# Fixed SBUF addresses for the operands of TensorE's products in a two-layer hybrid encoder

## The chip, the cores and the metric

The kernel runs on one core of one Trainium2 chip. The metric is the device time of one execution, in microseconds (us). The kernel before took 1218.03 us, the median of 3 runs (1217.06 to 1219.15).

## The reference, cut to what matters

The program is an encoder of two layers on 512 tokens of 1024 features, all in float32. Layer 0 mixes tokens with windowed attention (8 query heads, 2 key heads), layer 1 with a recurrent block (convolution, two gated scans, GELU gate). After each mixer comes a squared-ReLU MLP, and every sub-layer is wrapped in a modulation computed from `c` and a LayerNorm:

```python
def sq_relu_mlp(h, w1, w2):
    return jnp.square(jax.nn.relu(h @ w1)) @ w2
...
    y = sq_relu_mlp(x * (1.0 + scale) + shift, mlp_w1[i], mlp_w2[i])
    x = layer_norm(DN_ALPHA * x + (1.0 + gate) * y, ln_g[i, 1], ln_b[i, 1])
```

The two MLPs (1024 to 4096 to 1024) are most of the arithmetic.

## The kernel before

**Products in three passes.** TensorE multiplies in a rounded form of float32 (fp32r), so every float32 operand is split into a high part and a low part, and `mm3` (line 604) issues three matmuls for one product: high by high, high by low, low by high. Each matmul has a stationary operand, `lhsT`, of 128 partitions by 128 columns, which an LDWEIGHTS instruction loads, and a moving operand, `rhs`, of 128 partitions by up to 512 columns, which the MATMUL streams. A column is 4 bytes in each partition.

**Buffers.** Per partition of SBUF there are six weight buffers `w0` to `w5` (2048 columns: high parts, then low parts), four `raw` buffers into which weights land by DMA, `ht` (8192 columns: the modulated activations, transposed), `hid0` to `hid15` (512 columns each, used in pairs, high and low: the hidden activations), `xb0` to `xb3`, `rows` (6144 columns), `acc2`, fifteen `ex` buffers for temporaries, and some tens of small tiles.

**Order of the work.** A weight unit is 128 by 1024 values. `dma_unit` (line 543) loads it on SP's queue into a raw buffer, `conv_unit` (line 554) splits it with one ScalarE cast and one VectorE subtraction into a free `w` buffer. `m_tiles` (line 854) multiplies a unit, stationary, by `ht`, moving: 8 products, 24 matmuls. `out_tiles` (line 875) multiplies `hid` (in the attention and the recurrent block partly `ht`), stationary, by a unit, moving: again 24 matmuls per unit. An MLP goes four times through 8 units of the first kind and 8 of the second. Beside the first MLP run the matrix-vector products of the modulations (`gemv_tasks`, line 696): DMAs into the same raw buffers and long VectorE instructions.

**Who sets the order.** The kernel is written as a list of operations on symbolic tiles; `schedule` (line 330) is a planner that gives every operation a cost and an engine and puts all in one static order. It knows tiles by name and size; no address enters it. `emit` (line 468) then issues the operations in that order, and `real` (line 476) makes the actual tile at the moment when an operation first names it.

**Where the buffers lie.** The pool hands out SBUF addresses in the order in which tiles are made, each rounded up to 32 bytes, from byte 16512 on, which is 128 modulo 256. Tiles are made on first use, so small tiles of 4 to 512 bytes fall in between the large ones, and the large ones land on different addresses modulo 256. In the program of the kernel before these are:

| buffer | address modulo 256 |
|---|---|
| ht | 0 |
| w0, w3, w4, w5 | 192 |
| w1 | 32 |
| w2 | 128 |
| hid0, hid1 | 96 |
| hid2, hid3 | 192 |
| hid4, hid5 | 224 |
| hid6 to hid15 | 0 |

All slices that the products take inside a buffer begin at multiples of 512 bytes, so the distance between two operands modulo 256 is that of their buffers. In what follows the **distance** of a matmul is the address of the stationary operand that is loaded next, less that of the moving operand that is being streamed, modulo 256. The matmuls of the program and of the trace stand in the same order, so each record can be given its operands' addresses (the trace's names leave the buffer numbers out). For 512-column matmuls of 128 partitions that ran at full clock, the distances are as follows; "w by ht" is w stationary and ht moving, "hid by w" hid stationary and w moving; stretches are us from the start of the span:

| stretch, product | 192 | 0 | 32 | 64 | 96 | 128 | 160 | 224 |
|---|---|---|---|---|---|---|---|---|
| 13.7 to 61, w by ht | 119 | 0 | 48 | 0 | 0 | 24 | 0 | 0 |
| 61 to 219, w by ht | 44 | 0 | 0 | 0 | 0 | 0 | 0 | 0 |
| 61 to 219, hid by w | 0 | 10 | 22 | 28 | 0 | 0 | 17 | 11 |
| 219 to 392.6, w by ht | 171 | 0 | 70 | 0 | 0 | 49 | 0 | 0 |
| 219 to 392.6, hid by w | 11 | 24 | 35 | 205 | 2 | 24 | 23 | 57 |
| 392.6 to 418.8, w by ht | 47 | 0 | 24 | 0 | 0 | 24 | 0 | 0 |
| 418.8 to 558.9, w by ht | 177 | 0 | 24 | 0 | 0 | 47 | 0 | 0 |
| 418.8 to 558.9, hid by w | 11 | 36 | 29 | 135 | 2 | 23 | 35 | 66 |
| 558.9 to 616, w by ht | 72 | 0 | 0 | 0 | 0 | 0 | 0 | 0 |
| 558.9 to 616, hid by w | 0 | 0 | 4 | 35 | 2 | 0 | 1 | 2 |
| 616 to 861.9, w by ht | 263 | 0 | 73 | 0 | 0 | 95 | 0 | 0 |
| 616 to 861.9, hid by w | 5 | 1 | 1 | 52 | 18 | 27 | 0 | 28 |
| 861.9 to 1199.1, w by ht | 404 | 0 | 120 | 0 | 0 | 120 | 0 | 0 |
| 861.9 to 1199.1, hid by w | 5 | 60 | 60 | 361 | 28 | 84 | 94 | 49 |

The functions that the change touches, with their line numbers:

Of the kernel before, what the change touches and what calls it, by code (L numbers as in the profile page):

```python
# [9 lines left out]
F32 = mybir.dt.float32  # L10
# [223 lines left out]
class Program:  # L234
# [233 lines left out]
    def emit(self, nc, tc, pools):  # L468
        fix = lambda a: self.real(a, pools)
        with tc.manual_schedule():  # L470
            for op in self.schedule():
                args = [fix(a) for a in op.args]
                kw = {k: fix(a) for k, a in op.kw.items()}
                op.ins = getattr(getattr(nc, op.eng), op.fn)(*args, **kw)  # L474

    def real(self, a, pools):
        if not isinstance(a, View):
            return a
        t = a.tile
        if t.real is None:  # L480
            pool = pools[t.kind]
            shape = [1, t.n] if t.kind == "dr" else [128, t.n]
            tag = f"ps{t.bank}" if t.kind == "ps" else t.tag
            t.real = pool.tile(shape, F32, tag=tag, name=tag)
        return a.get()
# [1027 lines left out]
```

## Time and profile before

| | before |
|---|---|
| median of 3 runs | 1218.03 us |
| the profiled execution's own time | 1218.25 us |
| its span (first to last instruction) | 1216.5 us |
| TensorE matmuls, busy | 1148.1 us (94%), 5332 of them |
| TensorE weight loads, busy | 938.8 us (77%), beside the matmuls |
| VectorE busy | 871.3 us (72%) |
| ScalarE busy | 529.3 us (44%) |

How to read it: the span is 1.75 us shorter than the execution's own time, so a change of the span is a change of the time. TensorE is busy most of the time, but a matmul is pipelined: its record overlaps the next one's, so the time that one costs is the distance from its start to the start of the next (called its pitch here), not the duration that a row gives as the mean of one. In a timeline row of N matmuls in one piece, the piece's length is N-1 pitches and one last record. All lines stand as L474, since one helper issues every operation; names of tiles tell the work apart, buffer numbers left out.

### The profile page before, as it was taken

To read this page: it belongs to the slowest core of one execution; us is meant where nothing else is said; L and a number is where in the kernel's file an instruction comes from. 1 tells how busy PE (TensorE), PEld (TensorE's weight loads), DVE (VectorE), ACT (ScalarE), POOL (GpSimd) and SP (SyncE) were. 2 spreads that over 40 slices of the span, in tenths; PEclk is the share of its full clock that TensorE was granted. 3 is DMA by queue.
4 is the path that set the end of the run, shared out by engine and by line. 5 is a ranking of instruction groups with operands and counts; after the bars stand their busy time and mean duration, and the time that the engine had idled before them with its cause. 6 is when DMAs were issued, how large, how long until landed. Compare 5 with 4: busy or idle time off the path is not lost.

```text
span 1216.5 us, 14406 instructions
## 1 busy us (share of the span) xinstructions
PE 1148.1 (94%) x5332; PEld 938.8 (77%) x5332; DVE 871.3 (72%) x1303; ACT 529.3 (44%) x787; POOL 77.1 (6%) x47
## 2 busy tenths in 40 slices
PE   7987989999999899998999988979999999999996
PEld 5876767988888688887887866768888888888885
DVE  7898979978878785449948888689935444444447
ACT  4465664512322342424468889834431422322411
POOL 1000000022232220000000000000000000000004
PEclk9997999999999999999999989899999999999998
DMA  9866552367667753221232442443422222222201
GB/s 337 297 193 206 157 181 79 117 220 247 204 239 244 240 192 138 87 104 37 96 104 92 143 130 84 148 139 101 164 100 102 89 101 90 101 90 95 96 1 70
DMA packets 54140, 172.01 MB, mean 141 GB/s; under 512 B 7715, under 2 KB 8227, under 8 KB 54070
## 3 DMA queue, kind: packets, MB, share of 16 engines
q1 hardware_dynamic: 54070, 171.09, 42.0%
q8 instruction: 42, 0.69, 0.2%
q14 instruction: 28, 0.23, 0.1%
HBM read 160.56 MB, written 2.11 MB: 134 GB/s over the span
## 4 chain that ended last, share of the span: by engine, by line
PE 63%; DVE 19%; ACT 8%; DMA 7%; issue 2%; SPq 0%; DVEq 0%; ACTq 0%
PE ps L474 63%; DVE ex L474 5%; DVE w L474 4%; DVE rows L474 3%; DMA raw<-in_adaw 3%; DVE xb L474 2%; ACT rows L474 2%; ACT w L474 2%; DMA raw<-in_W 1%; DVE ht L474 1%; DVE acc L474 1%; DMA rows<-w 1%; ACT ex L474 1%; ACT L474 1%; DVE mv L474 1%
## 5 line engine op out<-in xcount | busy, mean ns | idle before, releaser
L474 PE MATMUL ps<-ht,w 128*128 128x512 f32 (+1 forms) x2664 | 557.0, 370 | 6.2 <-ACT w L474 3.9
L474 PEld LDWEIGHTS ps<-ht,w 128*128 128x128 f32 x2664 | 461.8, 190 | 96.6 <-ACT w L474 4.4
L474 PE MATMUL ps<-w,hid 128*128 128x512 f32 (+1 forms) x1800 | 422.7, 393 | 0.0
L474 DVE TENSOR_TENSOR w<-raw,w 128x1024 fp32r<-128x1024 f32 x192 | 240.5, 1257 | 228.9 <-ACT w L474 226.2
L474 PEld LDWEIGHTS ps<-w,hid 128*128 128x128 f32 x1800 | 335.7, 189 | 78.8 <-DVE rows L474 0.2
L474 ACT CAST w<-raw 128x1024 fp32r<-128x1024 f32 x192 | 198.6, 1042 | 429.7 <-PE ps L474 304.2
L474 PE MATMUL ps<-w,ht 128*128 128x512 f32 (+1 forms) x336 | 74.2, 371 | 6.3 <-DVE w L474 3.4
L474 PEld LDWEIGHTS ps<-w,ht 128*128 128x128 f32 x336 | 57.4, 193 | 18.2 <-DVE w L474 3.8
L474 DVE SCALAR_TENSOR_TENSOR ex<-rows,ps 128x512 f32<-128x512 f32 (+1 forms) x81 | 53.2, 672 | 22.0 <-PE ps L474 22.0
L474 DVE SCALAR_TENSOR_TENSOR acc<-raw,sc,acc 128x1024 f32<-128x1024 f32 x40 | 52.6, 1314 | 16.2 <-DMA raw<-in_adaw 15.9
L474 ACT ACTIVATE rows<-ps 128x512 f32<-128x512 f32 x66 | 39.1, 592 | 43.4 <-PE ps L474 41.9
L474 DVE SCALAR_TENSOR_TENSOR rows<-raw,sc,rows 128x1024 f32<-128x1024 f32 x40 | 53.8, 1346 | 4.9 <-DMA raw<-in_adaw 4.6
L474 DVE TENSOR_TENSOR xb<-xb,ex 128x512 f32<-128x512 f32 (+1 forms) x81 | 55.5, 698 | 0.6
L474 POOL TENSOR_TENSOR ex<-xb,rows 128x512 f32<-128x512 f32 x5 | 6.8, 1375 | 754.1 <-ACT xb L474 754.1
L474 DVE TENSOR_TENSOR hid<-ex,hid 128x512 fp32r<-128x512 f32 x66 | 47.5, 722 | 5.5 <-ACT hid L474 0.9
L474 DVE TENSOR_TENSOR ex<-rows 128x512 f32<-128x512 f32 x64 | 45.8, 715 | 5.4 <-ACT rows L474 5.4
L474 ACT ACTIVATE hid<-rows 128x512 fp32r<-128x512 f32 x64 | 40.5, 633 | 1.9
L474 PE MATMUL ps<-ex,w 96*128 96x512 f32 x108 | 31.5, 445 | 8.8 <-ACT ex L474 3.2
L474 PEld LDWEIGHTS ps<-ex,w 96*128 96x128 f32 x108 | 22.5, 214 | 16.8 <-ACT w L474 4.9
L474 DVE TENSOR_TENSOR rows<-rows,ex 128x512 f32<-128x512 f32 x32 | 21.6, 686 | 18.6 <-DMA rows<-rows 12.6
L474 ACT ACTIVATE xb<-xb,mv 128x512 f32<-128x512 f32 x29 | 22.2, 808 | 26.7 <-DVE mv L474 26.7
L474 PE MATMUL ps<-ident,ex 128*128 128x128 f32 x124 | 21.1, 285 | 10.9 <-DVE ex L474 9.8
(147 smaller groups left out, 830.0 us busy)
## 6 DMA issues: line engine op xcount, KB each, us to landing
raw<-in_W SPq DMA_DIRECT2D x184, 512.0 KB
raw<-in_adaw SPq DMA_DIRECT2D x80, 512.0 KB
ex<-in_ada0t SPq DMA_DIRECT2D x28, 256.0 KB
rows<-w SPq DMA_DIRECT2D x16, 192.0 KB
raw<-in_W SPq DMA_DIRECT2D x8, 288.0 KB
rows<-rows SPq DMA_DIRECT2D x36, 64.0 KB
xb<-in_xT SPq DMA_DIRECT2D x8, 256.0 KB
rows<-in_lnb SPq DMA_DIRECT2D x4, 512.0 KB
```

The source lines that it names most:

```text
L474: op.ins = getattr(getattr(nc, op.eng), op.fn)(*args, **kw)
```

## The change

Before it issues anything, the kernel now makes the large buffers in a fixed order, with three unused pads of 128, 192 and 192 bytes per partition between their groups. `place` looks up the first tile of each name in the planned order, and sets its `real`; `real()` finds it there later. Small tiles are made on first use as before, after all the large ones.

```diff
     def emit(self, nc, tc, pools):
         fix = lambda a: self.real(a, pools)
         with tc.manual_schedule():
-            for op in self.schedule():
+            order = self.schedule()
+            self.place(order, pools)
+            for op in order:
                 args = [fix(a) for a in op.args]
                 kw = {k: fix(a) for k, a in op.kw.items()}
                 op.ins = getattr(getattr(nc, op.eng), op.fn)(*args, **kw)
+
+    LAYOUT = (
+        [128, "ht", "rows", "acc2"]
+        + [f"ex{i}" for i in range(17) if i not in (12, 13)]
+        + [f"raw{i}" for i in range(4)]
+        + [192]
+        + [f"w{i}" for i in range(6)]
+        + [f"xb{i}" for i in range(4)]
+        + [192]
+        + [f"hid{i}" for i in range(16)]
+    )
+
+    def place(self, order, pools):
+        first = {}
+        for op in order:
+            for a in (*op.args, *op.kw.values()):
+                if isinstance(a, View) and a.tile.kind == "sb":
+                    first.setdefault(a.tile.tag, a.tile)
+        for i, what in enumerate(self.LAYOUT):
+            if isinstance(what, int):
+                pools["sb"].tile([128, what // 4], F32, tag=f"pad{i}", name=f"pad{i}")
+            else:
+                t = first[what]
+                t.real = pools["sb"].tile([128, t.n], F32, tag=what, name=what)
```

From byte 16512 the pad of 128 bytes ends at 16640, which is 0 modulo 256. All the large buffers are multiples of 256 bytes long, so `ht`, `rows`, `acc2`, the `ex` and the `raw` buffers begin at 0 modulo 256, the `w` and `xb` buffers at 192, and the `hid` buffers at 192 + 192 = 128.

## Rows read from the trace of the kernel before

**Rows 1.** The page: head, and busy time of TensorE's two parts and VectorE.

```profile
span 1216.5 us, 14406 instructions
...
PE 1148.1 (94%) x5332; PEld 938.8 (77%) x5332; DVE 871.3 (72%) x1303; ACT 529.3 (44%) x787; POOL 77.1 (6%) x47
```

**Rows 2.** The chain that ended last, its long TensorE pieces: start us, us, what.

```profile
13.73 47.31 PE ps L474 x192
...
219.00 173.06 PE ps L474 x814
...
418.83 140.00 PE ps L474 x596
...
590.46 25.52 PE ps L474 x144
...
861.90 337.21 PE ps L474 x1512
```

**Rows 3.** Windows by stretch: busy us (instructions) of each engine, granted clock, DMA.

```profile
core 0: us, PE busy (x) PEld busy (x) DVE busy (x) ACT busy (x) POOL busy (x), PEclk, DMA share, GB/s
...
61.00:219.00 158.00, 137.56 (x752) 113.97 (x751) 141.11 (x289) 88.92 (x187) 2.46 (x4) 0.94 0.49 159
219.00:392.60 173.60, 173.60 (x818) 143.61 (x819) 144.85 (x163) 51.30 (x67) 40.93 (x16) 1.00 0.67 218
...
558.90:616.00 57.10, 51.69 (x297) 44.49 (x296) 50.28 (x89) 23.11 (x34) 0.00 (x0) 0.97 0.24 78
616.00:861.90 245.90, 228.09 (x1017) 183.84 (x1016) 202.72 (x300) 179.28 (x262) 0.00 (x0) 0.97 0.38 119
861.90:1199.10 337.20, 337.20 (x1514) 275.97 (x1515) 164.17 (x213) 100.09 (x128) 5.50 (x4) 1.00 0.25 89
```

**Rows 4.** The page's costliest groups: the two kinds of matmul.

```profile
L474 PE MATMUL ps<-ht,w 128*128 128x512 f32 (+1 forms) x2664 | 557.0, 370 | 6.2 <-ACT w L474 3.9
...
L474 PE MATMUL ps<-w,hid 128*128 128x512 f32 (+1 forms) x1800 | 422.7, 393 | 0.0
```

**Rows 5.** TensorE's timeline, w by ht: start us, us, what, count of one piece.

```profile
33.07 21.91 PE L474 MATMUL ps<-ht,w 128*128 128x512 f32 x95
...
1126.39 21.91 PE L474 MATMUL ps<-ht,w 128*128 128x512 f32 x95
...
1148.36 5.53 PE L474 MATMUL ps<-ht,w 128*128 128x512 f32 x23
...
1153.96 5.73 PE L474 MATMUL ps<-ht,w 128*128 128x512 f32 x24
```

**Rows 6.** TensorE's timeline, hid by w: five pieces.

```profile
369.40 2.68 PE L474 MATMUL ps<-w,hid 128*128 128x512 f32 x11
...
895.59 2.71 PE L474 MATMUL ps<-w,hid 128*128 128x512 f32 x11
...
1015.43 5.75 PE L474 MATMUL ps<-w,hid 128*128 128x512 f32 x24
...
1087.52 5.29 PE L474 MATMUL ps<-w,hid 128*128 128x512 f32 x22
...
1101.23 14.16 PE L474 MATMUL ps<-w,hid 128*128 128x512 f32 x60
```

**Rows 7.** Waits in 392 to 420 us: who waited for whom, us, times, longest.

```profile
PE ps L474 <- ACT w L474: 3.9, 1, 3.9
ACT w L474 <- DMA raw<-in_W: 2.5, 1, 2.5
```

**Rows 8.** One short window behind that wait, columns as in rows 3.

```profile
419.20:422.50 3.30, 3.30 (x9) 2.36 (x8) 2.58 (x3) 0.00 (x0) 0.00 (x0) 0.50 0.87 252
```

**Rows 9.** The page's groups for splitting one weight unit.

```profile
L474 DVE TENSOR_TENSOR w<-raw,w 128x1024 fp32r<-128x1024 f32 x192 | 240.5, 1257 | 228.9 <-ACT w L474 226.2
L474 ACT CAST w<-raw 128x1024 fp32r<-128x1024 f32 x192 | 198.6, 1042 | 429.7 <-PE ps L474 304.2
```

**Rows 10.** TensorE's timeline, w by ht, one more piece.

```profile
519.32 5.53 PE L474 MATMUL ps<-ht,w 128*128 128x512 f32 x23
```

## The prediction

> **What bounds the kernel now.** I read the page first: TensorE is busy for 94% of the span, VectorE for 72% [rows 1]. A share says nothing of where the end is set, so next comes the chain of work that ended last. Its long pieces are TensorE's own: 47.3, 173.1, 140.0, 25.5 and 337.2 us in which matmul follows matmul and nothing else is waited for [rows 2]. In those 723 us a matmul that starts sooner after the one before moves the end; elsewhere (61 to 219 us, 616 to 861.9 us) TensorE has gaps and other engines lead [rows 3].
>
> Then, how far are matmuls apart? The page's mean of one, 370 or 393 ns, is a pipelined duration [rows 4]; the pitch comes from the timeline. A piece of N is N-1 pitches and a last record of about 0.39 us. For w by ht at distance 192 (w0, w3, w4, w5): (21.91 - 0.39)/94 = 228.9 ns, in the first stretch as in the last [rows 5]. The same product with w1, distance 32, which starts at 1148.36: 5.14/22 = 233.6 ns, where a rounding of 0.01 us is worth 0.5 ns; with w2, distance 128, from 1153.96: 5.34/23 = 232.2 ns [rows 5]. Nothing differs between these pieces but the slot. For hid by w the longest piece, 60 matmuls at distance 64, has 13.77/59 = 233.4 ns; distance 224 (w1 with hid8 to hid11) has 5.36/23 = 233.0; distance 128 (w2 with hid12 to hid15) has 4.90/21 = 233.3; distance 0 (w3 with hid2 and hid3) has 2.32/10 = 232. The telling piece is at 369.40 us: w1 with hid4 and hid5, 32 and 224, is by chance at distance 192, and its 11 matmuls have 2.29/10 = 229 ns [rows 6]. So one distance is 4.4 ns cheaper in both products, whichever operand is the weight and wherever the two lie.
>
> **The change part by part.**
>
> *Pads and order of making.* Three pads, 512 bytes, no instruction. The planner has finished before any address exists, so order, queues and waits are the same. Cost nil.
>
> *Weight buffers against ht.* ht stays at 0, w1 and w2 move to 192 like the others. All w by ht go to distance 192: those at 32 gain 233.4 - 229.0 = 4.4 ns (price of the longest piece), those at 128 gain 3.3.
>
> *hid against the weight buffers.* hid 128 less w 192 is 192 as well. Nearly all of these 1732 matmuls change. I price distances 32, 64, 96, 128, 160 and 224 at 4.4 ns (pieces between 233.0 and 233.4), and 0 at 1.6, about half of what its one short piece shows.
>
> *By stretch*, with the counts of the table of distances:
> - 861.9 to 1199.1: w by ht 120 x 4.4 + 120 x 3.3 = 0.92 us; hid by w 676 x 4.4 + 60 x 1.6 = 3.07; together 4.0.
> - 418.8 to 558.9: 24 x 4.4 + 47 x 3.3 = 0.26; 290 x 4.4 + 36 x 1.6 = 1.33; together 1.6.
> - 13.7 to 61: 48 x 4.4 + 24 x 3.3 = 0.3.
> - 219 to 418.8: (94 x 4.4 + 73 x 3.3) + (346 x 4.4 + 24 x 1.6) = 0.65 + 1.56 = 2.2.
> - 61 to 219, 558.9 to 616 and 616 to 861.9: 0.36 + 0.19 + 1.18 = 1.7.
>
> The whole is 9.8 us. The first three, 5.9, I count in full: TensorE leads the chain there. In the last of them VectorE is busy for 164 of 337 us and the DMA engines for a quarter [rows 3], so what splits the weights (1.26 us of VectorE and 1.04 of ScalarE per unit [rows 9], against 24 x 0.229 = 5.5 us of matmuls) still hides. From 219 to 418.8 I count half, 1.1: the stretch ends in a wait of TensorE for a weight unit, 3.9 us, behind a raw buffer whose DMA was late [rows 7], with VectorE busy for 145 of 174 us before [rows 3]. If the loads of the matrix-vector products set that wait, TensorE arrives earlier and waits longer; if what TensorE frees sets it, all is kept. In the last group I count a third, 0.6, since TensorE is idle for some 44 us of it [rows 3] and mostly waits for others. Sum 7.6; some ten matmuls after each change of product start off the cheap rhythm, so 7.5. Ends: 5.9 and 9.8.
>
> *What the rows don't show.* Half-width matmuls (614 of w by ht, 377 of them at 192 already) at other distances: zero, between -0.5 and +0.5 us if half of 4.4 ns goes either way for 237 of them. The other engines see new addresses too; the split ran over four raw and three kinds of w addresses, and no row separates them: zero, with 1% of VectorE's 203 us in 616 to 861.9 [rows 3], 2 us, either way. Granted clock: behind the wait at 418 us it was 0.50 for 3.3 us [rows 8], half speed, worth 1.7 us. A stall that moves may gain or lose one such stretch.
>
> *Rule against rows.* The rows have TensorE's pitch depend on where the two operands lie. The Trainium skill, "SBUF — State Buffer", section "SBUF: two separate sides", says that TensorE never waits on anyone for SBUF, and "TensorE: Matmul & The Clock Gate", Part 2, that a weight load doesn't take read bandwidth from the running matmul. By that the sum would be zero and the time 1218; the trace speaks against it, above all the piece at 369.40 us.
>
> **The rivals.**
>
> *A, slower: the expensive rhythm at distance 192.* The 23 matmuls from 519.32 us, w3 by ht, are at distance 192 and yet have 5.14/22 = 233.6 ns [rows 10]. So 192 allows the cheap rhythm and doesn't ensure it. Once all products share one distance, nothing breaks a rhythm for over a thousand matmuls; if the last stretches start in the expensive one, the 945 matmuls at 192 in the stretches that TensorE leads lose 4.4 ns (4.2 us, of which half of 1.0 is hidden before 418.8), and those at 128 and 0 lose 0.6: 1218.25 + 4.3 = 1222.5. It wins from 7.0/(7.0 + 4.3) = 62% of the matmuls on. For it: that piece. Against: it is one of 25 pieces of over ten matmuls at 192, and pieces of 95, over three changes of slot, hold 228.9 [rows 5].
>
> *B, half: it holds for w by ht alone.* For hid by w only 22 matmuls were ever at 192, in two pieces. If they were luck, w by ht gives 0.92 + 0.26 + 0.3 + half of 0.65 + a third of 0.63 = 2.0: 1216.2. Against: nothing sets the piece at 369.40 apart but the distance.
>
> *C, nothing.* The pitch follows something that goes with the slots and not the addresses, or the pool doesn't place tiles as asked: 1218.2. Against: the same pitch at 64 and at 32, with different pairs of buffers. The pages' rule above is this rival.
>
> **How the numbers follow.** The profiled execution took 1218.25 us, 0.2 above the median of the runs, 1218.03; against it the sum gives 1218.25 - 7.5, and I say 1210.7. Chances: forecast 0.82, A 0.06, B 0.06, C 0.06. The forecast's own range is from 1218.25 - 9.8 - 1.7 = 1207 to 1218.25 - 5.9 + 1.7 = 1214. I set it to hold nine in ten of its case (0.74), and go on to 1216.4 to take in B: 1207.0 to 1216.4 for 0.80. A difference of 0.2%, 2.4 us, is about what a measurement of this kernel tells from none. Faster by more: the forecast and half of B, less a little for a small gain, 0.84; within: C and some of B, 0.10; slower: A, 0.06.
>
> **What would show it.** Right: in the profile after, pieces of both products at 229 ns with every slot; the last long TensorE piece shorter by 4 us, the one from 418.8 by 1.6; TensorE's instructions and order unchanged, VectorE's and ScalarE's durations too. Half counted rightly: the wait before 418 us longer by 1 us. Wrong if hid by w stays at 233 (B), if long pieces at 192 have 233 (A), or if all pitches fall and the end doesn't, the gain lying in longer waits.

## The result, and the profile after

The changed kernel took 1210.84 us, the median of 6 runs (1209.32 to 1211.42); the kernel before, run beside it, 1218.51 us (6 runs). The ratio is 0.9926, with a 95% interval of 0.9912 to 0.9939: faster by 0.7%. The forecast was 1210.7 us. The profiled execution took 1211.31 us, 6.9 less than that of the kernel before.

The page of the changed kernel, head and busy times:

```profile
span 1209.5 us, 14406 instructions
...
PE 1142.6 (94%) x5332; PEld 942.0 (78%) x5332; DVE 872.3 (72%) x1303; ACT 528.5 (44%) x787; POOL 77.0 (6%) x47
```

Against [rows 1] the instructions are the same in number, VectorE and ScalarE are busy for as long as before to within 1 us, and the span is 7.0 us shorter. TensorE's matmuls went from 1148.1 us to 1142.6, its weight loads, which run beside them, from 938.8 to 942.0. The split of a weight unit is unmoved too, so the new addresses changed next to nothing on the other two engines:

```profile
L476 DVE TENSOR_TENSOR w<-raw,w 128x1024 fp32r<-128x1024 f32 x192 | 241.0, 1260 | 223.1 <-ACT w L476 220.7
...
L476 ACT CAST w<-raw 128x1024 fp32r<-128x1024 f32 x192 | 198.5, 1041 | 420.6 <-PE ps L476 305.2
```

(1260 and 1041 ns, where [rows 9] has 1257 and 1042.) Now the pitch. In the last MLP there is a piece of 192 matmuls of each product, eight units through all six slots. TensorE's timeline of the changed kernel (start us, us, what):

```profile
933.66 44.13 PE L476 MATMUL ps<-ht,w 128*128 128x512 f32 x192
977.62 44.11 PE L476 MATMUL ps<-w,hid 128*128 128x512 f32 x192
```

and the same two pieces of the kernel before:

```profile
937.77 44.31 PE L474 MATMUL ps<-ht,w 128*128 128x512 f32 x192
981.91 44.86 PE L474 MATMUL ps<-w,hid 128*128 128x512 f32 x192
```

Read as in the prediction, (44.13 - 0.39)/191 = 229.0 ns for w by ht, where a mixture of slots had 229.9, and 228.9 ns for hid by w, where the mixture had 232.8. These two pieces are the yardstick for all the experiments below.

The chain that ended last, its long TensorE pieces:

```profile
13.56 45.73 PE ps L476 x192
...
216.56 104.90 PE ps L476 x525
...
415.92 138.10 PE ps L476 x594
...
858.77 333.31 PE ps L476 x1512
```

Against [rows 2] the last, with the same 1512 matmuls, is 3.9 us shorter, the one after 415 us 1.9 (with two matmuls fewer), the first 1.6. The piece that was 173 us long is now 105: beyond it another engine is last in the chain though TensorE has no gap (in the profile of run 10 below, the same kernel, it is one piece again).

Windows over the stretches of the prediction, by the same matmuls (busy us and instructions of each engine, granted clock, DMA):

```profile
59.40:216.60 157.20, 136.37 (x751) 113.16 (x751) 140.97 (x289) 88.87 (x187) 2.46 (x4) 0.95 0.49 159
216.60:388.50 171.90, 171.90 (x819) 143.92 (x820) 144.71 (x162) 51.37 (x66) 40.86 (x16) 1.00 0.67 218
...
611.30:858.70 247.40, 231.03 (x1016) 187.25 (x1014) 202.59 (x300) 179.01 (x262) 0.00 (x0) 0.94 0.39 118
858.70:1192.10 333.40, 333.39 (x1515) 276.16 (x1515) 164.03 (x214) 99.95 (x129) 5.51 (x4) 1.00 0.27 90
```

The last stretch went from 337.2 to 333.4 us and the second of these from 173.6 to 171.9 [rows 3]. But the recurrent layer, 245.9 us before, now takes 247.4, and its granted clock fell from 0.97 to 0.94.

Laid beside each other matmul by matmul, the two traces differ by 6.9 us from the first matmul to the last. By what the pitches are: 8.4 us less in 512-column matmuls that waited for nothing, about 0.6 less in narrower ones, 0.9 less in waits, and 3.0 more in matmuls at half clock.

### The profile page after: what moved, and what is told of

The parts are those of the page before. It is cut to its first block, busy times and chain, and to the rows that moved or that the text cites. A ratio compares the mean times of both kernels' runs of the same rounds, so it can differ in the third digit from the quotient of the medians.

```text
span 1209.5 us, 14406 instructions
## 1 busy us (share of the span) xinstructions
PE 1142.6 (94%) x5332; PEld 942.0 (78%) x5332; DVE 872.3 (72%) x1303; ACT 528.5 (44%) x787; POOL 77.0 (6%) x47
## 4 chain that ended last, share of the span: by engine, by line
PE 57%; DVE 20%; ACT 8%; DMA 8%; issue 5%; POOL 2%; SPq 1%; DVEq 0%; ACTq 0%; POOLq 0%
PE ps L476 57%; DVE ex L476 5%; DVE w L476 5%; DVE rows L476 4%; DMA raw<-in_adaw 3%; DVE xb L476 2%; ACT rows L476 2%; ACT w L476 2%; POOL ex L476 2%; DMA raw<-in_W 1%; DMA rows<-w 1%; DVE ht L476 1%; DVE acc L476 1%; ACT ex L476 1%; ACT L476 1%
## 5 line engine op out<-in xcount | busy, mean ns | idle before, releaser
L476 PE MATMUL ps<-w,hid 128*128 128x512 f32 (+1 forms) x1800 | 415.2, 390 | 0.0
L476 DVE TENSOR_TENSOR w<-raw,w 128x1024 fp32r<-128x1024 f32 x192 | 241.0, 1260 | 223.1 <-ACT w L476 220.7
L476 ACT CAST w<-raw 128x1024 fp32r<-128x1024 f32 x192 | 198.5, 1041 | 420.6 <-PE ps L476 305.2
```

## The experiments

All kernels fix the large buffers as the change does. Where only pads differ, the diff is one or two lines. Unless it says otherwise the time is the median of 4 to 10 runs, and the ratio, with its 95% interval, is to the kernel before on the same chip.

**1. Both products at distance 64.**

```diff
-        + [192]
+        + [64]
         + [f"w{i}" for i in range(6)]
...
-        + [192]
+        + [64]
         + [f"hid{i}" for i in range(16)]
```

> The large buffers are fixed as in the change, but the pads are 128, 64 and 64 bytes, so both products lie at distance 64 in place of 192; ht, ex, rows and raw stay where the change puts them. Theory (the distance modulo 256 sets the pitch): 233.3 ns in both products with every slot; against the change 5.8 us lost in the last long TensorE piece, 2.5 in the one from 418 us, 1.7 before 418, 0.8 in the first, a third of the rest: about 1222, between 1219 and 1225, slower than before the change. Rival 1 (the gain comes from large buffers that begin at multiples of 64 or 256, for DMAs and the other engines, or from tiles lying together): 1211, as the change. Rival 2 (ht at 0 is what counts): w by ht stays at 229 ns, time about 1216.

1223.06 us, the kernel before 1220.40: 1.0027 of it (1.0010 to 1.0045), slower by 0.3%. The two pieces:

```profile
938.83 44.95 PE L476 MATMUL ps<-ht,w 128*128 128x512 f32 x192
983.62 44.96 PE L476 MATMUL ps<-w,hid 128*128 128x512 f32 x192
```

233.3 ns in both. The same fixed order, the same places for ht, ex, rows and raw, yet the gain is gone and more: it lies in the distance, not in large buffers that begin on round addresses or lie together. That is rival C's end.

**2. Only hid by w at 192, and 5. only w by ht at 192.** Pads 64 and 192, then 192 and 64, in the same two lines.

> Pads 128, 64 and 192: w by ht at distance 64, hid by w at 192. Theory: w by ht 233.3 ns, hid by w 229; against the change 2.7 us lost in the last long piece and 1.0 in the one from 418 us, 1217 in all, between 1214.5 and 1219. Rival (absolute places: the w buffers have to be at 192): hid by w at 233 too, 1222.

> Pads 128, 192 and 64: w by ht at distance 192, hid by w at 64; the counterpart of the run with hid by w alone. Theory: w by ht 229 ns, hid by w 233.3; against the change 3.1 us lost in the last long piece, 1.4 from 418 us, about 0.9 before 418: 1216.5, between 1214.5 and 1219. Rival B of the prediction (the distance matters for w by ht alone): hid by w as in the change, 1211.

The first took 1219.70 us (0.9999 of the kernel before, 0.9984 to 1.0014), 0.7 us over its range; the second 1217.76 (0.9987; 0.9973 to 1.0001), within it. Pieces of the first:

```profile
941.45 44.96 PE L476 MATMUL ps<-ht,w 128*128 128x512 f32 x192
986.24 44.13 PE L476 MATMUL ps<-w,hid 128*128 128x512 f32 x192
```

and of the second:

```profile
940.66 44.12 PE L476 MATMUL ps<-ht,w 128*128 128x512 f32 x192
984.62 44.96 PE L476 MATMUL ps<-w,hid 128*128 128x512 f32 x192
```

In these pieces each product follows its own distance: 229.0 ns at 192, 233.3 at 64, whatever the other does. Rival B, that hid by w wouldn't answer, is out. The miss of the first has a reason in its trace: over the whole run its hid by w had 230.6 ns on average, not 229, since 627 of some 1700 ran in the expensive rhythm at 192 (233 ns, rival A). Two whole pieces of the last stretch are among them:

```profile
896.65 44.96 PE L476 MATMUL ps<-w,hid 128*128 128x512 f32 x192
...
1075.01 44.96 PE L476 MATMUL ps<-w,hid 128*128 128x512 f32 x192
```

**3. Everything 64 bytes further.** First pad 192 in place of 128; ht at 64, w at 0, hid at 192.

> Pads 192, 192 and 192: every large buffer lies 64 bytes further, all distances as in the change (ht 64, w 0, hid 192). Theory: both products at 229 ns, time as the change, 1209.5 to 1213. Rival (absolute places count): pitches of 231 to 233 and 1215 or more.

1211.67 us, 0.9928 (0.9908 to 0.9949).

```profile
933.71 44.13 PE L476 MATMUL ps<-ht,w 128*128 128x512 f32 x192
977.68 44.11 PE L476 MATMUL ps<-w,hid 128*128 128x512 f32 x192
```

To 0.01 us the change's pieces. The absolute place doesn't count, as far as a shift of 64 bytes shows it.

**4. Distance 0.** Pads 256 and 256.

> Pads 128, 256 and 256: all large buffers at 0, distance 0 in both products. In the trace before, pieces at distance 0 had 229 and 232 ns, so the theory has 229 to 232 and a time between the change and 1218: about 1214. If it is 229 throughout, 192 is not the only cheap distance: 1211.

1203.53 us, 0.9857 (0.9835 to 0.9879): about twice the change's gain.

```profile
927.53 43.68 PE L476 MATMUL ps<-ht,w 128*128 128x512 f32 x192
971.05 43.68 PE L476 MATMUL ps<-w,hid 128*128 128x512 f32 x192
```

(43.68 - 0.39)/191 = 226.6 ns, in both products, less than either of the ends that I expected. So 192 was not the cheapest distance.

**6. Distance 0 without pads.** Both lines `[192]` between the groups left out, so that the distance is 0 modulo 512, where run 4 had 256.

> As the run at distance 0, but with no pads between the groups, so that the distance is 0 modulo 512 too, where it was 256 before. Theory (256 is the period): 226.8 ns in both products, about 1203.5, 1201 to 1206. Rival (the period is 512 or more): other pitches than 226.8 and a time off by over 3 us.

1205.96 us, 0.9884 (0.9861 to 0.9906), with pieces of 43.68 us again. 256 is the period as far as these two distances show; the intervals of 4 and 6 overlap.

**7 and 8. Scans.** Each weight buffer is made 64 columns longer and used from its own small offset:

```diff
+    SHIFT = {'w0': 4, 'w1': 8, 'w2': 16, 'w3': 24, 'w4': 48, 'w5': 0}
+    def make(self, t, pools):
+        o = self.SHIFT.get(t.tag)
+        n = t.n if o is None else t.n + 64
+        tile_ = pools["sb"].tile([128, n], F32, tag=t.tag, name=t.tag)
+        return tile_ if o is None else tile_[:, o // 4 : o // 4 + t.n]
```

The second scan has 80, 112, 144, 176, 208 and 12.

> No pads between the groups; each weight buffer gets its own small offset, so that w by ht has distances 4, 8, 16, 24, 48 and 0 in slots w0 to w5, and hid by w 252, 248, 240, 232, 208 and 0. One look at the pitches. Theory: each slot has its own pitch, 226.8 ns in w5, rising towards 233 within some tens of bytes. Rival (cheap only on exact equality, or cheap in steps of 16 or 32 bytes): 233 already at 4, or 226.8 up to a step. The time, a mixture, about 1210.

> The same with w by ht at distances 80, 112, 144, 176, 208 and 12 in w0 to w5, hid by w at 176, 144, 112, 80, 48 and 244. Theory: pitches between 229 and 236 ns, lowest at those nearest to 192 (176 and 208, about 230), with w5 near 227 to 230. Rival (192 is one exact point): 176 and 208 at 233 like the others. About 1216.

One run each: 1219.06 and 1218.25 us, the first 9 over what I expected, the second 2. Mean pitches in ns of stretches at one distance, without the first six matmuls of each, from the records (the kernel before adds 32, 64, 128 and 192):

| distance | 0 | 4 | 8 | 12 | 16 | 24 | 32 | 48 | 64 | 80 | 112 |
|---|---|---|---|---|---|---|---|---|---|---|---|
| w by ht | 226.8 | 232.4 | 230.7 | 232.2 | 233.3 | 230.5 | 233.3 | 233.3 | | 232.1 | 233.3 |
| hid by w | 227.1 | | | | | | 233.1 | 234.7 | 233.4 | 231.8 | 233.3 |

| distance | 128 | 144 | 176 | 192 | 208 | 232 | 240 | 244 | 248 | 252 |
|---|---|---|---|---|---|---|---|---|---|---|
| w by ht | 232.1 | 233.4 | 230.3 | 229.0 | 231.9 | | | | | |
| hid by w | 233.0 | 230.3 | 231.1 | 229.6 | 230.3 | 233.3 | 231.8 | 228.9 | 233.7 | 237.0 |

The picture of a smooth valley fell. 0 is a narrow point: in the scan, four bytes beside it the pitch is 5 to 10 ns higher (run 12 adds a case where it is 1 ns higher). 192 isn't one exact point: 176 and 208 have 230.3 to 231.9, so the rival for it is out. But a valley around it isn't shown either: 8, 24 and, for hid by w, 144 lie in the same range (230.3 to 230.7), and hid by w has 228.9 at 244. In the scans each distance belongs to one weight buffer, and the 229.6 of hid by w at 192 rests on 10 matmuls. I could name no order in these values.

**9. Which two operands?** The low parts of ht, hid and w0 to w4 moved by 128 bytes against their high parts.

```diff
+            if gap:
+                rows, cols = op[1]
+                if (cols.start or 0) >= self.tile.n // 2:
+                    cols = slice(cols.start + 32, cols.stop + 32)
+                v, gap = v[rows, cols], False
...
-        + [f"hid{i}" for i in range(16)]
+        + [f"hid{i}" for i in range(0, 16, 2)] + [128] + [f"hid{i}" for i in range(1, 16, 2)]
```

> Which pair of operands counts? All high parts at distance 0, and the low parts of ht, of hid and of w0 to w4 moved by 128 bytes (w5 keeps its low part in place). In the order high by high, high by low, low by high, the weight load that runs beside each matmul is then at distance 0 from the operand being streamed, while the stationary operand of the matmul itself lies 128 from the moving one in two matmuls of three. Theory (the load of the next stationary against the stream): 226.8 ns in w0 to w4, in both products, and more in w5, where one or two of three loads are at 128. Rival (a matmul's own two operands): 230 ns or more in w0 to w4.

One run, 1215.88 us.

```profile
935.66 44.64 PE L482 MATMUL ps<-ht,w 128*128 128x512 f32 x192
980.14 44.54 PE L482 MATMUL ps<-w,hid 128*128 128x512 f32 x192
```

231.7 and 231.2 ns over the six slots; in w0 to w4 alone, 231.1 and 231.0 by the records. My theory said 226.8, and it fell: that the load running beside a matmul is at distance 0 from that matmul's stream isn't enough. The rival's 230 or more came. It isn't proved by it: the matmul's own operands may count, or both pairs, or a distance that alternates may break the rhythm. In every other kernel the two pairs have the same distance, so there the distance as used here can stand for both; which of the two counts stays open.

**10 and 11. The change and distance 0 on one chip.** Both as above, run again.

> The changed kernel once more, beside the next run on the same chip: 0.993 of the kernel before, about 1211 if that has 1219.

> The kernel with all large buffers at distance 0 once more: 226.8 ns against 229.1 on some 3700 matmuls, of which TensorE leads in some 2500: 6 to 8 us under the change, 0.986 to 0.988 of the kernel before. If the earlier gap came from the chip and not the distance, less than 3 us.

The change 1210.45 us, 0.9931 (0.9916 to 0.9946); distance 0 1204.51, 0.9880 (0.9861 to 0.9899). They are 5.9 us apart, against 6 to 8 expected and far from the rival's 3, with pieces of 44.13 and 43.68 us as before. Their intervals don't meet: distance 0 is the better layout.

**12. The weights 252 bytes on.** The offset of the scans, 252 for all six slots.

> The layout at distance 0, with all six weight buffers moved by 252 bytes: w by ht at distance 252, hid by w at 4. The scan had 237 ns for hid by w at 252 and 232.4 for w by ht at 4. Theory (the distance sets the pitch in both products alike, and the pitch the time): w by ht 237 ns, hid by w 232 to 237; against the kernel at distance 0 20 us or more lost, of which some 11 in the last long piece: 1226, between 1221 and 1232, slower than before the change. Rival (what the fixed layouts gained came mostly from something else): under 1218.

1215.65 us, 0.9969 (0.9953 to 0.9985). By the number the rival won; the pieces say why:

```profile
935.17 44.97 PE L476 MATMUL ps<-ht,w 128*128 128x512 f32 x192
979.97 43.88 PE L476 MATMUL ps<-w,hid 128*128 128x512 f32 x192
```

w by ht at 252 has 233.4 ns and hid by w at 4 has 227.7, where the scan had 237.0 for hid by w at 252 and 232.4 for w by ht at 4. Close to 0 the price doesn't carry over from one product to the other, and the theory's first half, one pitch for both, fell. What does hold is that the pitch makes the time: in the last stretch the 644 w by ht lose 6.6 ns against distance 0 and the 741 hid by w 1.1, 4.3 + 0.8 = 5.1 us, and the two traces differ there by 5.2.

## Why the prediction was right, point by point

**The price of a distance: right.** Both products came to 229 ns with every slot, from pieces of 95 and of 11 matmuls in the trace before [rows 5, 6]. Runs 1, 2, 3 and 5 show that the distance does it, and in each product by itself.

**The sum: right, with parts that don't repeat.** One profile is one execution. Run 10 is the changed kernel again, and run 3 has the same distances, so their traces tell how firm a part is. The chain that ended last in run 10, its long TensorE pieces:

```profile
11.88 47.00 PE ps L476 x192
...
218.02 171.15 PE ps L476 x814
...
415.67 139.05 PE ps L476 x596
...
857.15 334.63 PE ps L476 x1512
```

Gains by stretch in us, from the start of the same matmul to the start of the same matmul, each against the one trace before:

| stretch (of the trace before) | counted | the change | run 10 | run 3 |
|---|---|---|---|---|
| 13.7 to 61 | 0.3 | 1.6 | 0.3 | 0.9 |
| 219 to 418.8 | 1.1 | 1.2 | 2.2 | 2.7 |
| 418.8 to 558.9 | 1.6 | 1.1 | 1.0 | 0.1 |
| 861.9 to 1199.1 | 4.0 | 3.9 | 2.6 | 2.6 |
| 61 to 219, 558.9 to 861.9 | 0.6 | -1.0 | -0.6 | 0.6 |

The columns add up to 7.6, 6.8, 5.5 and 6.9 us. Run 10, whose profiled execution was 7.2 us shorter than that of the kernel before, got 1.9 of them ahead of the first product (it starts at 11.88 us in place of 13.73 [rows 2]), where none of the products has run yet.

**The last long piece, 4.0 us: right.** 3.9. The pitch gave 3.9 in all three traces; in run 10 and run 3 some 1.3 of it went to matmuls at half clock at the start of the stretch. **From 418.8 us, 1.6: a little high.** The same matmuls took 1.1 us less: 1.4 from the pitch and 0.3 lost at half clock; the rest of the pitch went to rival A, below.

**219 to 418.8 us, half of 2.2: met by the change's profile, not by the other two.** In the former TensorE was 1.9 us ahead at the wait and 1.2 after it. The wait of 3.9 us [rows 7] kept its length and got company; waits of 388 to 417 us in the changed kernel (us in total, times, longest):

```profile
ACT w L476 <- DMA raw<-in_W: 11.2, 5, 4.2
...
PE ps L476 <- ACT w L476: 3.9, 1, 3.9
...
PE ps L476 <- DVE w L476: 0.7, 1, 0.7
```

ScalarE waited 11.2 us for loads of weights there, 2.5 before [rows 7]. But in run 10 it waited 9.1 us and in run 3 8.3, while TensorE's wait was one of 3.9 and one of 3.3 us and all of the pitch's gain was kept. So it isn't shown that the loads set that wait, and the sign that I named, a wait longer by 1 us, came in one profile of three.

**61 to 219 and 558.9 to 861.9 us, a third of 1.7 kept: not found.** They took 1.0 us more. The term that came out wrong is that for granted clock, which I put into the range and not the sum. Pitches and waits gave gains in the recurrent layer (0.4 and 1.4 us), but matmuls at half clock cost 3.8. Two such windows of the changed kernel:

```profile
661.90:665.30 3.40, 3.40 (x10) 2.66 (x9) 3.40 (x5) 2.91 (x6) 0.00 (x0) 0.50 0.57 160
808.70:815.50 6.80, 5.65 (x13) 4.46 (x14) 3.46 (x5) 1.49 (x2) 0.00 (x0) 0.50 0.25 80
```

The clock before had none at the first place and 3.4 us at the second. They stand behind waits of TensorE, as that of [rows 8] does, and where they fall differed between profiles of one kernel: run 10, the change again, has 3.4 us at the second. With 0.6 us lost in run 10 and 0.6 gained in run 3, neither a gain nor a loss is shown for these stretches. **The first stretch, 0.3: too small in this profile.** It gained 1.6, of which 1.1 is the clock: seven of the first matmuls ran at 427 ns before and at full clock after. In run 10 they are at 427 ns again, and the gain is 0.3.

So in the change's profile one term of the 7.5 was 1.3 too low and another 1.6 too high. That they cancel to 6.9 us is luck, and so is the forecast's hit to 0.1 us: the medians of the two kernels lie 7.7 us apart, and single stretches move by 1 to 2 us from one execution to the next. What the traces support is the pitch's part, and a sum of 5.5 to 6.9 us from the first product on.

Two readings of the prediction are off without touching the sum. The table of distances counts 1723 hid by w, not 1732. And the piece at distance 0 [rows 6] isn't the only one, see below.

**Rival A, the expensive rhythm: real, and smaller than its worst.** The changed kernel's timeline has two long pieces of it at distance 192:

```profile
420.13 12.06 PE L476 MATMUL ps<-ht,w 128*128 128x512 f32 x51
...
713.45 32.60 PE L476 MATMUL ps<-ht,w 128*128 128x512 f32 x139
```

(12.06 - 0.39)/50 and (32.60 - 0.39)/138 are both 233.4 ns. The first starts behind the wait at 415 us and ends with its product. With two shorter pieces some 216 matmuls lose 4.4 ns each, 0.95 us: most of the 1.4 that lack between the 9.8 us of pitch that I summed and the 8.4 found in 512-column matmuls. In the last stretch of this profile it never came. In run 2 it did, in two pieces of 192 there, and in run 10 some 65 matmuls in all had it. What starts it no run shows.

**Distance 0: misread.** I took 1.6 ns of gain left from one piece of 11 matmuls with 232 ns. The trace before has ten pieces of 12 at that distance: without their first six matmuls, four have 226.7 ns and six 230.2. The first value is what runs 4, 6 and 11 hold over whole products, so a better distance than 192 could be suspected there, though not told from the trace before alone.

**The pages' rule.** The Trainium skill, "SBUF — State Buffer", section "SBUF: two separate sides", has TensorE wait on no one for SBUF. Runs 1 and 4 differ in pads alone and by 6.7 ns in the pitch of both pieces, so the sum isn't zero, as it would be by that rule, and the measurement decides. Why the addresses matter, and whether the weight load has a part in it, run 9 leaves open.

## What to carry to other kernels

Where TensorE leads, list the pitch of matmuls by the relative address of their two operands modulo 256: a kernel with scattered buffers has already run the experiment. Put large operands at fixed places, the same modulo 256, and measure the pitch over pieces of a hundred matmuls, since pieces of a dozen gave 226.7 or 230.2 ns at one and the same distance. Count the gain in full only where TensorE leads the chain, and expect a per cent to be blurred by where half-clock stretches fall.

## What was not expected

- Distance 0 is a single point: 226.8 ns, and four bytes beside it 232.4 (w by ht at 4), 237.0 (hid by w at 252), 233.4 (w by ht at 252) or 227.7 (hid by w at 4).
- At distance 192 there are two rhythms, 229 and 233.4 ns, and a product kept the one it started in over pieces of up to 192 matmuls; at distance 0 no long piece was in a second one.
- Half-width matmuls (256 columns, w by ht) have the opposite order: 114.7 ns at distance 64 (run 1), 117.8 at 192 (run 3), 119.8 at 0 (run 4). Narrower matmuls took some 2 us more in run 4 than in the change's trace that way, most of it where TensorE doesn't lead. A layout with both at their best wasn't tried.
